# Seven-product up-projection: pads off POOL, sums a product ahead, another order of products, first weights loaded in the last output tile

## The chip, the cores and the metric

The kernel runs on one core of a Trainium2 chip. The metric is the device time of one execution in microseconds (us), the median of several runs. A core has TensorE (PE in the profile, with PEld for its weight loads), VectorE (DVE), ScalarE (ACT), GpSimd (POOL) and SyncE (SP, which here only issues DMAs). Each engine works through its own instructions in order and waits on semaphores for the others.

## The reference, cut to what matters

The kernel computes one layer of a hybrid decoder: a mixer (a state-space part and a convolution part side by side), then a gated MLP with a causal depthwise convolution of width 3. The change touches the last step of the mixer (its output projection) and the up-projection of the MLP.

```python
def rmsnorm(x, w):
    xf = x.astype(jnp.float32)
    r = lax.rsqrt(jnp.mean(xf * xf, axis=-1, keepdims=True) + EPS)
    return (xf * r).astype(x.dtype) * w
...
def conv_ffn(h, buf0, w_up, conv_w, conv_b, w_down):
    u = h @ w_up                                    # 2048 -> 2 x 5504
    u, buf = causal_dwconv(u, buf0, conv_w, conv_b) # width 3, along the tokens
    g, v = jnp.split(u, [FFN_DIM], axis=-1)
    return (jax.nn.silu(g) * v) @ w_down, buf
...
    out = jnp.concatenate([y.astype(h.dtype), u], axis=-1) @ w_out   # last step of mixer
...
        xp = xp + m
        f, p_ffc = conv_ffn(rmsnorm(xp, norm_ffn_w[i]), p_ffc0, *ffn_w)
        xp = xp + f
```

There are 544 tokens: 512 of one prompt and 8 x 4 of running samples. All is in float32.

## The kernel before

**Stages.** Input projection and mixer (to about 1015 us), the output projection of the first half (to 1217), of the second half, `ou`, in 16 tiles (to 1410.7), the up-projection (to 2425.6), and the down-projection. Every matmul stands for three: weights and activations are split into a high part (a cast, on ScalarE) and a low part (source minus high part, on VectorE), and TensorE runs high x high, high x low and low x high (L1246 to L1248 in the up-projection).

**Up-projection.** The hidden size has 43 groups (HID) of 128 columns of gate and 128 of value. A group is a 2 x 2 block problem (gate and value by the two halves of the input dimension, against the two halves of the tokens) worked with seven products in place of eight, each of 8 k-tiles x 3 passes = 24 matmuls with 272 columns. Product q = 7g+m wants a weight tile of 128x1024 and the operands T_t[m, k], which are sums of the normalised activations.

- *Weights.* `load_w(g, j)` loads five raw tiles a group, j = 0 to 4, each by one DMA of SP (L1198); j = 1 and 2 are sums of two blocks, so a second DMA, on POOL's queue, adds the other block once the first has landed (L1200). There are five buffers (`wr`). `prep_sum` makes the sixth tile, `ws` = raw 1 + raw 0 (L1211), and later adds raw 3 to it (L1213). `prep_h` casts a tile to its high part `sh` on ScalarE (L1221), `prep_l` makes the low part `sl` on VectorE (L1230); both have three buffers.
- *Operands.* `t_first` to `t_fourth` make T for one k: a split of the activations (`Ta`), of a difference (`tr`, L1130), of another (L1137), and of the second half (L1112, `Th` and `Tl`). For k = 0 to 4 (NPRE = 5) they run during the `ou` tiles, for k = 5, 6, 7 when the up-projection starts.
- *Behind a product.* `evac` adds its result from PSUM (four banks) into the group's tiles `c1`, `c2`, `pu`. `conv_task(g-1, m)` spreads the convolution of the group before over the seven iterations: at m = 0 and 2 `conv_in` for gate and value (two pads on POOL, L1279 and L1280; the normalisation factor `rr` or `nr` applied on VectorE, L1281 and L1282; the first tap on ScalarE, L1284), at 1 and 4 the other taps on VectorE, at 2 the silu on ScalarE, at 5 the product `ra` on VectorE and its store to DRAM (`ad`).

**What sets the order.** The order is written by hand: each engine's queue has the instructions in the order in which the loop over q emits them. An iteration before the change is

```python
            prep_sum(q + 2)
            prep_h(q + 2)
            if q:
                evac(q - 1)
            conv_task(q // 7 - 1, q % 7)
            prep_l(q + 2)
            ...
            product(q)
```

so the weights are prepared two products ahead. During the `ou` tiles, `delay(n, f)` and the steps that `ou_evac` returns place work between the weight blocks of the following tile; `swap` opens a pool of buffers in the place of one that is finished.

**The normalisation factor** of the MLP is not needed by the products. Its sum over the activations comes from a short TensorE step after the last `ou` tile; then `rv` (L243), a root, a reciprocal (L246) and three small steps follow on VectorE, before the first `conv_in` of the up-projection wants `rr`.

Of the kernel before, what the change touches and what calls it, by code (L numbers as in the profile page):

```python
# [9 lines left out]
F32R = mybir.dt.float32r  # L10
AF = mybir.ActivationFunctionType
ALU = mybir.AluOpType
# [4 lines left out]
KD = 16  # L17
HID = 43
KB = 4
NSLOT = 77  # L20
NSIDE = 10
CHUNKS = [14, 13, 12, 4]
U_SPILL = 8
# [6 lines left out]
def hymba_step_kernel(ctx: ExitStack, tc: tile.TileContext, a: dict):  # L30
# [236 lines left out]
    with tc.manual_schedule():  # L267
# [733 lines left out]
        def ln_gen():  # L1001
# [33 lines left out]
            def fin(t):  # L1035
                u = U_t.pop(t)

                def f1():
                    Uh[t] = slot("Uh", dt=F32R, side=t >= 12)
                    S.copy(Uh[t], u)  # L1040

                def f2():
                    Ul[t] = slot("Ul", dt=F32R, side=t >= 12)
# [83 lines left out]
        def t_second(k):  # L1127
            p, q = xs[k], xs[k + 8]
            r = tr[k] = slot("tr")
            V.tensor_tensor(r[:, 1, :], p[:, 0, :], p[:, 1, :], ALU.subtract)  # L1130
            V.scalar_tensor_tensor(r[:, 0, :], r[:, 1, :], -1.0, q[:, 1, :], ALU.mult, ALU.subtract)
            t_pair(k, r, (1, 2))

        def t_third(k):
            p, q = xs[k], xs[k + 8]
            r, s = tr.pop(k), slot("tr")
            V.tensor_tensor(s[:, 0, :], q[:, 1, :], p[:, 1, :], ALU.subtract)  # L1137
            V.scalar_tensor_tensor(s[:, 1, :], r[:, 0, :], -1.0, q[:, 0, :], ALU.mult, ALU.subtract)
            t_pair(k, s, (3, 6))

        def t_fourth(k):
            t_pair(k, xs.pop(k + 8), (4, 5))
            xs.pop(k)

        T_STEPS = [t_first, t_second, t_third, t_fourth]
        NPRE = 5

        def ou_evac(i):
            t = OT[i]

            def go(ps):
# [9 lines left out]
                def s1():  # L1161
# [7 lines left out]
                steps = [s0, s1]  # L1169
# [7 lines left out]
        run_jobs()  # L1177

        whl = swap("whl", "wp", bufs=1)
        wr = swap("wr", "side1", bufs=1, side="right")
        pst = swap("pst", "pmm", bufs=4, space=bass.MemoryType.PSUM)
        KW = 8 * 128
        fcw = cload("fcw", [128, 86, 4])
        fstate = []
        raw = {}

        def load_w(g, j):
            if g >= HID:
# [7 lines left out]
                G.dma_start(out=t, in_=more, accum_op=ALU.add)  # L1200
            raw[g, j] = t

        wq = {}

        def prep_sum(q):
            g, m = divmod(q, 7)
            if g >= HID:
                return
            if m == 1:
                raw[g, 5] = wr.tile([128, KW], F32, tag="s", bufs=1, name=nm("ws"))  # L1210
                V.tensor_tensor(raw[g, 5], raw[g, 1], raw[g, 0], ALU.add)  # L1211
            if m == 5:
                V.tensor_tensor(raw[g, 5], raw[g, 5], raw[g, 3], ALU.add)  # L1213

        def prep_h(q):
            g, m = divmod(q, 7)
            if g >= HID:
                return
            src = raw[g, (0, 5, 1, 2, 3, 5, 4)[m]]
            h = whl.tile([128, KW], F32R, tag="h", bufs=3, name=nm("sh"))  # L1220
            S.copy(h, src)  # L1221
            wq[q] = (src, h)

        def prep_l(q):
            g, m = divmod(q, 7)
            if g >= HID:
                return
            src, h = wq[q]
            l = whl.tile([128, KW], F32R, tag="l", bufs=3, name=nm("sl"))
            V.tensor_tensor(l, src, h.bitcast(F32), ALU.subtract)  # L1230
            wq[q] = (h, l)
            nxt = {1: (0,), 2: (1,), 3: (2,), 5: (3,), 6: (4,)}.get(m, ())
            for j in nxt:
                load_w(g + 1, j)

        bank = {}

# [14 lines left out]
        def evac(q):  # L1252
# [3 lines left out]
            c1, c2, pu = cg[g]  # L1256
            o = bank.pop(q)[:, 0:NH]
            if m == 0:
                S.copy(c1[:, 0, :], o)
            elif m == 1:  # L1260
                V.tensor_tensor(pu[:, 0, :], o, c1[:, 0, :], ALU.add)
            elif m == 2:
                V.tensor_tensor(pu[:, 1, :], o, pu[:, 0, :], ALU.add)
            elif m == 3:
                V.tensor_tensor(c2, o.unsqueeze(1).to_broadcast([128, 2, NH]), pu, ALU.add)
            elif m == 4:
                V.tensor_tensor(c1[:, 0, :], o, c1[:, 0, :], ALU.add)
# [24 lines left out]
        def conv_task(g, i):  # L1292
# [9 lines left out]
            elif i == 2:  # L1302
                o = cw[g][1]
                q = cw[g] = slot("gq", [128, 576])
                S.activation(q[:, 0:560], o[:, 0:560], AF.Silu)
                conv_in(HID + g, cg.pop(g)[1], R["nr2"])
            elif i == 4:
                conv_taps(HID + g)
# [7 lines left out]
                store(a_dram[g], flat(r))  # L1316

        NQ = 7 * HID
        for j in range(5):
            load_w(0, j)  # L1320
# [4 lines left out]
        rest = range(NPRE, 8)  # L1325
        for k in rest:
            if k == 7:
                prep_h(0)
                prep_l(0)
                drain_later()  # L1330
            t_first(k)
        prep_sum(1)
        for q in range(NQ):
            if q == 0:
                prep_h(1)
                prep_l(1)
                for k in rest:
                    t_second(k)
            tick()
            prep_sum(q + 2)  # L1340
            prep_h(q + 2)
            if q:
                evac(q - 1)
            conv_task(q // 7 - 1, q % 7)
            prep_l(q + 2)
            if q == 1:
                for k in rest:
                    t_third(k)
            if q == 2:
                for k in rest:  # L1350
                    t_fourth(k)
            product(q)
        evac(NQ - 1)
        T_t.clear()
# [273 lines left out]
```

## Time and profile before

| | before |
|---|---|
| median of 3 runs | 2981.86 us (2979.32 to 2982.01) |
| the profiled execution | 2978.53 us |
| its span | 2976.8 us |
| PE busy | 2875.1 us, 97% of the span |
| PEld busy | 2808.5 us, 94% |
| DVE busy | 1916.6 us, 64% |
| ACT busy | 1139.3 us, 38% |
| POOL busy | 902.3 us, 30% |
| weight loads of the up-projection, SP | 215 of 512 KB |
| accumulating weight loads, POOL | 86 of 512 KB |

A share of the span is a mean over stages: POOL's time lies for the most part ahead of the up-projection. Matmuls overlap in the array, so a matmul's own duration (about 0.29 us) is longer than its share of the time; how fast TensorE is going is read from how many start in a stretch. In rows of the trace the time in brackets is how long the engine stood idle ahead of the row, and what ended that.

### The profile page before, as it was taken

How to read it: one execution, taken by the hardware profiler on the slowest of the kernel's cores; microseconds unless marked ns; L12 is line 12 of the kernel's file. 1: busy time of each engine (PE TensorE's matmuls, PEld its weight loads, DVE VectorE, ACT ScalarE, POOL GpSimd, SP SyncE). 2: the span in 40 equal slices, each digit the busy share in tenths (PEclk: the TensorE clock that was granted, in tenths of full speed). 3: DMA queues.
4: the chain of work that ended last, by engine and by line, in shares of the span. 5: the costliest groups of instructions: out<-in, count | busy, mean ns of one | idle time of the engine just before them, and what ended most of it. 6: DMA issues, size and time to landing. Idle time of an engine off the chain costs nothing. (4 is left out here: it accounts for less than half of the span.)

```text
span 2976.8 us, 55786 instructions
## 1 busy us (share of the span) xinstructions
PE 2875.1 (97%) x22502; PEld 2808.5 (94%) x22502; DVE 1916.6 (64%) x2826; ACT 1139.3 (38%) x1682; POOL 902.3 (30%) x1068
## 2 busy tenths in 40 slices
PE   8999999999999999999899999999999989999997
PEld 8999999999999999999799999999999989999997
DVE  7576656777777874343777777777777774232334
ACT  5545434333333334233343434343434343232224
POOL 4567667666666655111001000010001000000003
PEclk9999999999999999999899999999999999999999
DMA  4243344333333344443566666676666655343421
GB/s 161 81 127 95 95 133 130 106 103 104 104 95 94 117 139 141 133 133 111 155 170 179 177 170 172 178 178 175 171 180 178 174 171 170 109 133 86 150 85 61
DMA packets 196677, 403.44 MB, mean 136 GB/s; under 512 B 38337, under 2 KB 47169, under 8 KB 196417
## 3 DMA queue, kind: packets, MB, share of 16 engines
q1 hardware_dynamic: 184032, 354.78, 38.7%
q0 software_dynamic: 12384, 45.09, 8.5%
q8 instruction: 176, 2.88, 0.4%
q14 instruction: 85, 0.69, 0.1%
HBM read 357.37 MB, written 42.41 MB: 134 GB/s over the span
## 5 line engine op out<-in xcount | busy, mean ns | idle before, releaser
L117 ACT CAST wh<-raw 128x512 fp32r<-128x512 f32 x592 | 355.6, 603 | 867.1 <-PE mm L228 735.0
L1248 PE MATMUL st<-Th,sl 128*128 128x272 f32 x2064 | 608.0, 295 | 32.6 <-DVE sl L1230 32.0
L1246 PE MATMUL st<-Th,sh 128*128 128x272 f32 x2064 | 604.1, 293 | 19.6 <-ACT sh L1221 17.6
L1247 PE MATMUL st<-Tl,sh 128*128 128x272 f32 x2064 | 599.6, 290 | 0.8 <-DVE Tl L1112 0.8
L118 POOL TENSOR_TENSOR wl<-raw,wh 128x512 fp32r<-128x512 f32 x336 | 449.4, 1340 | 416.9 <-ACT wh L117 356.5
L228 PE MATMUL mm<-xh,wh 128*128 128x272 f32 x2304 | 487.8, 293 | 7.3 <-ACT xh L312 7.3
L228 PE MATMUL mm<-xl,wh 128*128 128x272 f32 x2304 | 479.9, 289 | 3.2 <-DVE xl L314 3.2
L228 PE MATMUL mm<-xh,wl 128*128 128x272 f32 x2304 | 479.1, 289 | 0.0
L1248 PEld LDWEIGHTS st<-Th,sl 128*128 128x128 f32 x2064 | 391.8, 190 | 51.4 <-DVE sl L1230 51.2
L1246 PEld LDWEIGHTS st<-Th,sh 128*128 128x128 f32 x2064 | 391.9, 190 | 28.9 <-ACT sh L1221 27.2
L118 DVE TENSOR_TENSOR wl<-raw,wh 128x512 fp32r<-128x512 f32 (+2 forms) x256 | 181.2, 709 | 351.9 <-ACT wh L117 349.1
L1247 PEld LDWEIGHTS st<-Tl,sh 128*128 128x128 f32 x2064 | 392.2, 190 | 1.3 <-DVE Tl L1112 1.2
L228 PEld LDWEIGHTS mm<-xh,wh 128*128 128x128 f32 x2304 | 366.0, 189 | 20.0 <-issue 10.4
L228 PEld LDWEIGHTS mm<-xl,wh 128*128 128x128 f32 x2304 | 365.8, 189 | 4.1 <-DVE xl L314 4.0
L228 PEld LDWEIGHTS mm<-xh,wl 128*128 128x128 f32 x2304 | 366.1, 189 | 0.0
L1200 POOL DMA_DIRECT2D wr<-in_w_up x86 | 74.9, 871 | 899.7 <-DMA wr<-in_w_up 418.5
L937 DVE SCALAR_TENSOR_TENSOR ax<-w,cfw,ax 128x512 f32<-128x512 f32 x448 | 302.1, 746 | 5.8 <-ACT ax L913 5.8
L228 PE MATMUL mm<-Ah,wh 128*128 128x272 f32 x1248 | 260.0, 289 | 8.0 <-ACT Ah L1111 7.9
L1230 DVE TENSOR_TENSOR sl<-wr,sh 128x1024 fp32r<-128x1024 f32 x215 | 261.8, 1218 | 0.6 <-ACT sh L1221 0.6
L228 PE MATMUL mm<-Al,wh 128*128 128x272 f32 x1248 | 259.8, 289 | 0.0
L228 PE MATMUL mm<-Ah,wl 128*128 128x272 f32 x1248 | 259.7, 289 | 0.0
L1230 DVE TENSOR_TENSOR sl<-ws,sh 128x1024 fp32r<-128x1024 f32 x86 | 105.4, 1225 | 209.3 <-ACT sh L1221 209.3
(299 smaller groups left out, 5107.2 us busy)
## 6 DMA issues: line engine op xcount, KB each, us to landing
wr<-in_w_up SPq DMA_DIRECT2D x215, 512.0 KB, 3.9
raw<-in_w_in SPq DMA_DIRECT2D x292, 256.0 KB, 3.2
wr<-in_w_up POOLq DMA_DIRECT2D x86, 512.0 KB, 7.9
raw<-in_w_down SPq DMA_DIRECT2D x144, 256.0 KB, 2.7
raw<-in_w_out SPq DMA_DIRECT2D x128, 256.0 KB, 2.9
ad<-ra SPq DMA_DIRECT2D x43, 272.0 KB, 4.5
ar<-ad SPq DMA_DIRECT2D x43, 272.0 KB, 4.2
h<-in_h SPq DMA_DIRECT2D x32, 256.0 KB, 3.7
```

Source lines behind the costliest of these rows:

```text
L117: S.copy(h[:, :n], r[:, :n])
L118: (cur["wl"] or eng).tensor_tensor(l[:, :n], r[:, :n], h[:, :n].bitcast(F32), ALU.subtract)
L228: T.matmul(o, lhsT=w[:, c], rhs=x[:, hf, :], start=first, stop=last)
L937: V.scalar_tensor_tensor(p, w[:, i:i + 512], wt(i), p, ALU.mult, ALU.add)
L1200: G.dma_start(out=t, in_=more, accum_op=ALU.add)
L1230: V.tensor_tensor(l, src, h.bitcast(F32), ALU.subtract)
L1246: T.matmul(out, lhsT=h[:, c], rhs=xh_, start=k == 0, stop=False)
L1247: T.matmul(out, lhsT=h[:, c], rhs=xl_, start=False, stop=False)
L1248: T.matmul(out, lhsT=l[:, c], rhs=xh_, start=False, stop=k == 7)
```

## The change

Five things change. The pads of `conv_in` are a memset on VectorE and a copy on ScalarE, no longer on POOL. The two sums into `ws` are emitted behind `prep_l`, one iteration before the cast that reads them. The products of a group use the raw tiles in the order 0, 3, `ws`, 1, 2, `ws`, 4 (before: 0, `ws`, 1, 2, 3, `ws`, 4), with the operands and evictions renumbered, and the second `conv_in` goes from m = 2 to m = 3. The loads of the next group are issued at other places. In the last `ou` tile the weight buffers are opened on the place of another pool (`side0`, for which the layer norm's tiles are finished in another order), the five first loads are issued there, and the operands for k = 5 and 6 are made there.

```diff
-            for t in range(16):
+            for t in list(range(U_SPILL, 16)) + list(range(2, U_SPILL)) + [0, 1]:
+                if t == 0:
+                    Cur.side = swap("side0", "side1", bufs=4, side="right")
                 fin(t)
...
                 if i + 1 < 16:
                     load_xr(i + 1)
+                else:
+                    delay(0, up_open)
+                    delay(0, lambda: (t_first(5), t_fourth(5)))
+                    delay(1, lambda: (t_second(5), t_third(5)))
+                    delay(1, lambda: (t_first(6), t_fourth(6)))
+                    delay(2, lambda: (t_second(6), t_third(6)))
...
-            t_pair(k, r, (1, 2))
+            t_pair(k, r, (2, 3))
...
+        def up_open():
+            nonlocal wr
+            wr = swap("wr", "side0", bufs=1, side="right")
+            for j in (0, 1, 3, 2, 4):
+                load_w(0, j)
...
-            if m == 1:
+        def sum_a(g):
+            if g < HID:
                 raw[g, 5] = wr.tile([128, KW], F32, tag="s", bufs=1, name=nm("ws"))
                 V.tensor_tensor(raw[g, 5], raw[g, 1], raw[g, 0], ALU.add)
-            if m == 5:
-                V.tensor_tensor(raw[g, 5], raw[g, 5], raw[g, 3], ALU.add)
+                load_w(g + 1, 0)
+
+        def sum_b(g):
+            V.tensor_tensor(raw[g, 5], raw[g, 5], raw[g, 3], ALU.add)
+            load_w(g + 1, 3)
...
-            src = raw[g, (0, 5, 1, 2, 3, 5, 4)[m]]
+            src = raw[g, (0, 3, 5, 1, 2, 5, 4)[m]]
...
-            nxt = {1: (0,), 2: (1,), 3: (2,), 5: (3,), 6: (4,)}.get(m, ())
-            for j in nxt:
-                load_w(g + 1, j)
+            if m in (3, 4, 6):
+                load_w(g + 1, {3: 1, 4: 2, 6: 4}[m])
...
-            G.memset(w[:, 0:2], 0.0)
-            G.tensor_copy(ws[:, :, 0:2], fstate[t // 29][:, t % 29, :].rearrange("p (b x) -> p b x", x=2))
+            V.memset(w[:, 0:2], 0.0)
+            S.copy(ws[:, :, 0:2], fstate[t // 29][:, t % 29, :].rearrange("p (b x) -> p b x", x=2))
...
+            elif i == 3:
                 conv_in(HID + g, cg.pop(g)[1], R["nr2"])
...
         for q in range(NQ):
+            g, m = divmod(q, 7)
+            tick()
             if q == 0:
-                prep_h(1)
+                t_fourth(7)
                 prep_l(1)
-                for k in rest:
-                    t_second(k)
-            tick()
-            prep_sum(q + 2)
+                t_second(7)
+                sum_a(0)
             prep_h(q + 2)
             if q:
                 evac(q - 1)
-            conv_task(q // 7 - 1, q % 7)
+            conv_task(g - 1, m)
             prep_l(q + 2)
             if q == 1:
-                for k in rest:
-                    t_third(k)
-            if q == 2:
-                for k in rest:
-                    t_fourth(k)
+                t_third(7)
+                xs.clear()
+            if m == 2:
+                sum_b(g)
+            if m == 6:
+                sum_a(g + 1)
             product(q)
```

How the instructions stand on three engines, before and after. On ScalarE, in a steady group, from the eviction of a product to the casts behind the second convolution's first tap (`gq` is the silu, `o` the convolution, `w` its padded input), before:

```order
L1259 COPY c_18711<-st_18684 128x272
L1221 CAST sh_18747<-wr_18539 128x1024
L1305 ACTIVATE gq_18750<-o_18673 128x560
L1284 ACTIVATE o_18753<-w_18752,fcw_16760 128x560
L1221 CAST sh_18788<-ws_18634 128x1024
L1221 CAST sh_18820<-wr_18573 128x1024
```

and with the change:

```order
L1263 COPY pu_18460<-st_18430 128x272
L1226 CAST sh_18494<-wr_18247 128x1024
L1309 ACTIVATE gq_18497<-o_18422 128x560
L1226 CAST sh_18533<-ws_18389 128x1024
L1284 COPY w_18536<-fs_16875 128x8x2
L1288 ACTIVATE o_18537<-w_18536,fcw_16871 128x560
L1226 CAST sh_18570<-wr_18323 128x1024
```

The cast of the second `ws` now stands ahead of the first tap `o`, where it stood behind it, and the pad's copy stands in ScalarE's own queue.

On VectorE, in a steady group, around the first sum, from the product `ra` of the group before on, before:

```order
L1314 TENSOR_TENSOR ra_18858<-gq_18750,o_18753 128x2x256
L1315 TENSOR_TENSOR ra_18858<-gq_18750,o_18753 128x2x16
L1230 TENSOR_TENSOR sl_18861<-wr_18641,sh_18855 128x1024
L1211 TENSOR_TENSOR ws_18888<-wr_18681,wr_18641 128x1024
L1269 TENSOR_TENSOR c_18711<-st_18863,pu_18713 128x272
L1230 TENSOR_TENSOR sl_18893<-ws_18888,sh_18890 128x1024
L1271 TENSOR_TENSOR c_18712<-st_18897,c_18712 128x272
L1281 TENSOR_TENSOR w_18926<-c_18711,rr_17005 128x512
L1282 TENSOR_TENSOR w_18926<-c_18711,rr_17005 128x8x4
```

and with the change:

```order
L1319 TENSOR_TENSOR ra_18608<-gq_18497,o_18537 128x2x256
L1320 TENSOR_TENSOR ra_18608<-gq_18497,o_18537 128x2x16
L1235 TENSOR_TENSOR sl_18611<-wr_18391,sh_18605 128x1024
L1273 TENSOR_TENSOR c_18458<-st_18613,pu_18460 128x272
L1235 TENSOR_TENSOR sl_18641<-wr_18505,sh_18638 128x1024
L1213 TENSOR_TENSOR ws_18643<-wr_18466,wr_18391 128x1024
L1275 TENSOR_TENSOR c_18459<-st_18647,c_18459 128x272
L1283 MEMSET w_18675 128x2
L1285 TENSOR_TENSOR w_18675<-c_18458,rr_17011 128x512
L1286 TENSOR_TENSOR w_18675<-c_18458,rr_17011 128x8x4
L1235 TENSOR_TENSOR sl_18682<-ws_18643,sh_18672 128x1024
L1294 SCALAR_TENSOR_TENSOR o_18676<-w_18675,fcw_16871,o_18676 128x560 x2
```

The sum was followed at once by the split `sl<-ws` that needs it by way of ScalarE; now an eviction and a convolution's first steps stand between, and the split of raw 0 precedes the sum.

On SP, at the end of the `ou` tiles (`xs` are stores of the residual, `fcw` and `fs` the convolution's weights and states), before:

```order
L179 DMA xs_179<-xres_16250 128x544
L179 DMA xs_172<-xres_16380 128x544
L89 DMA fcw_16760<-in_fcw 128x344
L1198 DMA wr_16805<-in_w_up 128x1024
L1198 DMA wr_16807<-in_w_up 128x1024
L1198 DMA wr_16810<-in_w_up 128x1024
L1198 DMA wr_16813<-in_w_up 128x1024
L1198 DMA wr_16815<-in_w_up 128x1024
L1324 DMA fs_16817<-in_ffn_state 128x464
```

and with the change:

```order
L179 DMA xs_179<-xres_16297 128x544
L1205 DMA wr_16722<-in_w_up 128x1024
L1205 DMA wr_16724<-in_w_up 128x1024
L1205 DMA wr_16727<-in_w_up 128x1024
L1205 DMA wr_16729<-in_w_up 128x1024
L1205 DMA wr_16732<-in_w_up 128x1024
L179 DMA xs_172<-xres_16427 128x544
L89 DMA fcw_16871<-in_fcw 128x344
L1337 DMA fs_16873<-in_ffn_state 128x464
```

The five weight loads moved ahead of one store and of the convolution weights.

## Rows read from the trace of the kernel before

**Rows 1.** Busy times by stretch: length, each engine (instructions), clock, DMA share, GB/s.

```profile
1410.75:1461.30 50.55, 34.36 (x178) 31.30 (x178) 33.17 (x47) 17.65 (x25) 4.68 (x6) 0.76 0.57 155
1461.30:2425.60 964.30, 923.88 (x7057) 897.57 (x7055) 751.61 (x1051) 394.59 (x462) 90.20 (x252) 1.00 0.66 171
2402.70:2425.60 22.90, 22.90 (x182) 22.69 (x181) 18.06 (x26) 8.65 (x10) 2.14 (x4) 1.00 0.13 38
```

**Rows 2.** TensorE's waits from 1461.3 to 2425.6: total us, times, longest.

```profile
PE st L1248 <- DVE sl L1230: 28.9, 39, 0.7
PE st L1246 <- ACT sh L1221: 10.2, 27, 0.8
```

**Rows 3.** Timeline around the wait at 1824: start, us, engine, line [idle before].

```profile
1820.89 0.51 POOL L1280 COPY w<-fs 128x16 f32<-128x16 f32 x1
...
1821.28 0.85 ACT L1284 ACTIVATE o<-w,fcw 128x560 f32<-128x560 f32 x1 [6.15 <-POOL w L1280]
...
1822.04 1.03 ACT L1221 CAST sh<-ws 128x1024 fp32r<-128x1024 f32 x1
...
1824.38 0.40 PE L1248 MATMUL st<-Th,sl 128*128 128x272 f32 x1 [0.74 <-DVE sl L1230]
```

**Rows 4.** Timeline of the last group, 2412 to 2421.

```profile
2413.09 0.86 ACT L1284 ACTIVATE o<-w,fcw 128x560 f32<-128x560 f32 x1 [1.04 <-issue]
...
2418.25 1.63 DVE L1290 SCALAR_TENSOR_TENSOR o<-w,fcw,o 128x560 f32<-128x560 f32 x2
...
2419.80 1.22 DVE L1230 TENSOR_TENSOR sl<-wr,sh 128x1024 fp32r<-128x1024 f32 x1
```

**Rows 5.** Timeline of TensorE at the start of the up-projection.

```profile
1413.92 0.59 PE L1246 MATMUL st<-Ta,sh 128*128 128x272 f32 x1 [3.17 <-ACT sh L1221]
...
1426.25 0.59 PE L1246 MATMUL st<-Th,sh 128*128 128x272 f32 x1 [5.86 <-ACT sh L1221]
...
1456.80 0.40 PE L1248 MATMUL st<-Th,sl 128*128 128x272 f32 x1 [1.87 <-DVE sl L1230]
...
1461.06 0.30 PE L1248 MATMUL st<-Th,sl 128*128 128x272 f32 x1
```

**Rows 6.** Timeline of VectorE at the start of the up-projection.

```profile
1400.80 0.69 DVE L118 TENSOR_TENSOR wl<-raw,wh 128x512 fp32r<-128x512 f32 x1 [1.33 <-ACT wh L117]
...
1410.79 0.72 DVE L1156 TENSOR_TENSOR xres<-mm,xres 128x544 f32<-128x544 f32 x1 [9.30 <-PE mm L228]
...
1413.90 1.23 DVE L1230 TENSOR_TENSOR sl<-wr,sh 128x1024 fp32r<-128x1024 f32 x1 [0.47 <-ACT sh L1221]
...
1423.84 1.22 DVE L1211 TENSOR_TENSOR ws<-wr,wr 128x1024 f32<-128x1024 f32 x1 [8.36 <-DMA wr<-in_w_up]
...
1427.37 0.44 DVE L1130 TENSOR_TENSOR tr<-xs 128x272 f32<-128x272 f32 x1
...
1429.64 0.43 DVE L1130 TENSOR_TENSOR tr<-xs 128x272 f32<-128x272 f32 x1
...
1444.66 1.99 DVE L1112 TENSOR_TENSOR Tl<-xs,Th 128x544 fp32r<-128x544 f32 x3
...
1446.57 0.78 DVE L243 TENSOR_SCALAR rv<-ax 128x272 f32<-128x272 f32 x2
```

**Rows 7.** VectorE's one memset: us in total, mean ns, idle before.

```profile
L304 DVE MEMSET ones<- 128x128 f32 x1 | 0.2, 165 | 0.8 <-PEq L1617 0.8
```

**Rows 8.** L1198 and then L1200, 1500 to 2400: landing times and issue ns.

```profile
DMA to landing us min/median/max: 3.5/3.9/9.7
...
L1200 POOL DMA_DIRECT2D wr<-in_w_up x78: 862/865/888, 1517.4 to 2393.8; - x78
...
DMA to landing us min/median/max: 6.6/8.0/9.5
```

**Rows 9.** Timeline of SP's queue at the end of the last output tile.

```profile
1400.40 12.16 SPq L1198 DMA_DIRECT2D wr<-in_w_up  x5
```

**Rows 10.** The layer norm's step on `U`: ns min/median/max, first and last start.

```profile
L1045 DVE TENSOR_TENSOR U<-U,rr x16: 708/1261/1889, 1108.2 to 1153.7; 128x544 f32<-128x544 f32 x16
```

More of the change, by code (lines that the diff above doesn't have):

```diff
@@ L19 @@
 KB = 4
-NSLOT = 77
+NSLOT = 76
 NSIDE = 10
@@ L1038, in f1 @@
                 def f1():
-                    Uh[t] = slot("Uh", dt=F32R, side=t >= 12)
+                    Uh[t] = slot("Uh", dt=F32R, side=t < 2)
                     S.copy(Uh[t], u)
                 def f2():
-                    Ul[t] = slot("Ul", dt=F32R, side=t >= 12)
+                    Ul[t] = slot("Ul", dt=F32R, side=t < 2)
                     V.tensor_tensor(Ul[t], u, Uh[t].bitcast(F32), ALU.subtract)
@@ L1138, in t_third @@
             V.scalar_tensor_tensor(s[:, 1, :], r[:, 0, :], -1.0, q[:, 0, :], ALU.mult, ALU.subtract)
-            t_pair(k, s, (3, 6))
+            t_pair(k, s, (4, 6))
         def t_fourth(k):
-            t_pair(k, xs.pop(k + 8), (4, 5))
-            xs.pop(k)
-        T_STEPS = [t_first, t_second, t_third, t_fourth]
+            t_pair(k, xs[k + 8], (1, 5))
+        T_STEPS = [t_first, t_fourth, t_second, t_third]
         NPRE = 5
@@ L1168, in s1 @@
                         spawn(rsqrt_gen([fst["acc"], sq], setr("r2")), 3)
-                steps = [s0, s1]
+                steps = [s0, s1] if i < 15 else [lambda: None, s0, s1]
                 if i % 2 and i // 2 < NPRE:
@@ L1176, in hymba_step_kernel @@
             job("ou", out_srcs(OT[i], 1), lambda k: (Uh[k], Ul[k]), ou_evac(i), V, ou_pre(i))
[L1177 to L1185, printed above, removed]
         KW = 8 * 128
-        fcw = cload("fcw", [128, 86, 4])
-        fstate = []
-        raw = {}
+        raw, wq, wr = {}, {}, None
+        def up_open():
[3 more added lines that the diff above has]
+                load_w(0, j)
         def load_w(g, j):
@@ L1201, in load_w @@
             raw[g, j] = t
[L1203 to L1208, printed above, removed]
-            if m == 1:
+        def sum_a(g):
+            if g < HID:
                 raw[g, 5] = wr.tile([128, KW], F32, tag="s", bufs=1, name=nm("ws"))
                 V.tensor_tensor(raw[g, 5], raw[g, 1], raw[g, 0], ALU.add)
-            if m == 5:
-                V.tensor_tensor(raw[g, 5], raw[g, 5], raw[g, 3], ALU.add)
+                load_w(g + 1, 0)
+        def sum_b(g):
+            V.tensor_tensor(raw[g, 5], raw[g, 5], raw[g, 3], ALU.add)
+            load_w(g + 1, 3)
         def prep_h(q):
@@ L1258, in evac @@
             if m == 0:
-                S.copy(c1[:, 0, :], o)
+                S.copy(pu[:, 0, :], o)
             elif m == 1:
-                V.tensor_tensor(pu[:, 0, :], o, c1[:, 0, :], ALU.add)
+                V.tensor_tensor(c1[:, 0, :], o, pu[:, 0, :], ALU.add)
             elif m == 2:
+                V.tensor_tensor(pu[:, 0, :], o, pu[:, 0, :], ALU.add)
+            elif m == 3:
                 V.tensor_tensor(pu[:, 1, :], o, pu[:, 0, :], ALU.add)
-            elif m == 3:
+            elif m == 4:
                 V.tensor_tensor(c2, o.unsqueeze(1).to_broadcast([128, 2, NH]), pu, ALU.add)
-            elif m == 4:
-                V.tensor_tensor(c1[:, 0, :], o, c1[:, 0, :], ALU.add)
             elif m == 5:
@@ L1318, in hymba_step_kernel @@
         NQ = 7 * HID
-        for j in range(5):
-            load_w(0, j)
+        run_jobs()
+        whl = swap("whl", "wp", bufs=1)
+        pst = swap("pst", "pmm", bufs=4, space=bass.MemoryType.PSUM)
+        prep_h(0)
+        prep_l(0)
+        drain_later()
+        t_first(7)
+        prep_h(1)
+        fcw = cload("fcw", [128, 86, 4])
+        fstate = []
         for i in range(3):
@@ L1324, in hymba_step_kernel @@
             Y.dma_start(out=fstate[i][:, 0:n, :], in_=a["ffn_state"][:, 29 * i:29 * i + n, :])
-        rest = range(NPRE, 8)
-        for k in rest:
[L1327 to L1332, printed above, removed]
         for q in range(NQ):
+            g, m = divmod(q, 7)
+            tick()
             if q == 0:
-                prep_h(1)
+                t_fourth(7)
                 prep_l(1)
-                for k in rest:
-                    t_second(k)
-            tick()
-            prep_sum(q + 2)
+                t_second(7)
+                sum_a(0)
             prep_h(q + 2)
@@ L1343, in hymba_step_kernel @@
                 evac(q - 1)
-            conv_task(q // 7 - 1, q % 7)
+            conv_task(g - 1, m)
             prep_l(q + 2)
             if q == 1:
-                for k in rest:
-                    t_third(k)
-            if q == 2:
-                for k in rest:
-                    t_fourth(k)
+                t_third(7)
[4 more added lines that the diff above has]
+                sum_a(g + 1)
             product(q)
```

## The prediction

> **What bounds the kernel now.** I read first the busy times of stretches, because TensorE is the bound nearly everywhere and a mean over the span hides where it is not. Product 6 of group 0 issues its last matmul at 1461.06 [rows 5]; from there to 2425.6, in 42 groups, TensorE issues 42 x 168 = 7056 matmuls in 964.3 us, 22.96 us a group [rows 1]. In the last group, which has no further weights to load, 182 matmuls fill 22.90 us without a gap, 0.1258 us each [rows 1]. At that rate a group needs 21.14 us and the 7056 need 887.8. So the stretch **loses 76.5 us**, 1.82 a group. The chip grants the full clock there (1.00, its 2.4 GHz level) [rows 1].
>
> The waits of TensorE say for what: 28.9 us (39 times) for the low part of a weight tile from VectorE, 10.2 us (27 times) for the high part from ScalarE [rows 2]. They sum to 39.1, about half of the count's loss; the other half has no row of its own, and I take it to be the restart behind each stop and the clock that follows it. The count is what I use, and the other reading is a rival below.
>
> Next, one stop along the chain. At 1824.38 TensorE waits 0.74 for `sl` of the low pass [rows 3]. ScalarE cast the high part `sh<-ws` at 1822.04 only, because it had stood 6.15 us in front of the first step of the second convolution, which waits for POOL [rows 3]. POOL ran that pad copy at 1820.89 [rows 3]: its queue is in order, and an accumulating weight DMA ahead of it had first to see the plain load land. ScalarE's cast is late, VectorE's subtraction is late, TensorE stops. The cross-check is the last group, where POOL has no DMA left: the same step of ScalarE waited 1.04, and for nothing that the profile shows [rows 4].
>
> **The transition.** Group 0 costs 50.55 us for the first window, of which TensorE is busy 34.36 at a clock of 0.76 between the two levels [rows 1]. Its stops are 3.17 at the start, 5.86 before product 1 and 1.87 at the end, among smaller ones [rows 5]. VectorE's rows tell why: it sits 8.36 us until the accumulated weight tile lands at 1423.84, then makes the operands for k=5, 6, 7 one after another (second steps 2.27 us apart, 1427.37 to 1429.64), and reaches `rv` only at 1446.57 [rows 6]; the `sl` of product 6, behind the reciprocal that follows `rv`, lets TensorE go on at 1456.80 [rows 5].
>
> **The change, part by part, steady groups.** (1) Pads: POOL loses a memset and a copy per convolution and keeps only DMA issues. VectorE gets two memsets a group, at most 0.165 us each by the larger 128x128 one [rows 7]; ScalarE two copies, each below the 0.85 us of the much larger 128x560 activation [rows 3]. ScalarE is busy 394.59 / 42 = 9.4 us a group and VectorE 751.61 / 42 = 17.9 [rows 1]; they become at most 11.1 and 18.2 of 21.14. Both stay under TensorE, which hides them. Without that cover the two memsets would cost 0.33 us a group, 14 us in all. What stood behind POOL's DMA wait is now behind nothing: the cast `sh<-ws` follows in ScalarE's order only an activation whose operands VectorE has made. (2) Sums one product ahead: in one iteration ScalarE no longer waits for the sum it is to cast; same instructions, another place, so no price. (3) The second convolution's start moves from iteration 2 to 3, to even VectorE out. The longest iteration becomes the one with two taps: taps to the end of the next split take 2.77 us from 2418.25 [rows 4], with an eviction of 0.35 to 0.43 ahead (an estimate from the spacing of 128x272 steps [rows 6]) 3.1, against 3.02 a product. VectorE leads by two products, so the others (about 2.3 to 2.7) make it up: I find no split that is ready less than about 2.9 us before its product. The 76.5 should go wholly; I keep 15 us of it back for the range.
>
> (4) Later loads. The load of the second block comes after its split in iteration 1, one product later than before, and the first sum is wanted earlier. Counting from the end of product 0: load issued at 2.5 (two taps and a split, some 2.7, begun a little earlier), landing 3.9 (3.5 to 9.7), POOL's issue 0.87, accumulation landing 8.0 (6.6 to 9.5) [rows 8]: there at 15.2. The sum is wanted at 17.4 (five products, 15.1, and an eviction and a split behind them); TensorE suffers only if it begins after 21.8 (product 2 of the next group starts at 8 x 3.02 = 24.2, and sum and cast take 2.3). That leaves 6.6 us at the medians; if all worst cases met, 2.5 + 9.7 + 0.9 + 9.5 = 22.6, late by 0.8. VectorE is busy 78% of the stretch now [rows 1], and the landing times were measured beside that; it will be 86%. A rule speaks against the change here: the Trainium skill, "SBUF — State Buffer", section "SBUF: two separate sides", warns that descriptors which POOL writes can starve while VectorE holds the port they share. By that rule the accumulation would land later the busier VectorE is, and the last rival would be the likelier case, with its time. No row shows a starved issue (862 to 888 ns [rows 8]), and by the rows the cost is nothing.
>
> **The transition after.** The first weights are issued after one store in the last output tile, not over 12.16 us from 1400.40 on, where SP waited for buffers [rows 9]; the order shows five loads ahead of the store, the convolution weights and the states. Operands for k=5 and 6 are made in the last output tile, where VectorE has run its last weight step at 1400.80 and idles until 1410.79 [rows 6]. Four second and third steps at 2.27 and two short ones, some 11.4 us from 1401.5, end about 1413, so this does not quite fit: product 0 starts near 1413.0 (now 1413.92 [rows 5]), its low part near 1414.3. From the first split (1413.90) to `rv` (1446.57) VectorE now takes 32.7 us [rows 6]. Off come the wait of 8.36, four steps of 2.27 = 9.1, and two of the three last splits, 2 x 0.66 = 1.3 (1.99 for three [rows 6]); on come what is now behind the first split, the tile's eviction and the split of k=7, 3.1 to 3.6 (1410.79 to 1413.90 [rows 6]). That gives 17.0 to 17.5, with late ends up to 19: the first split starts near 1413.2, so `rv` near 1430.5 to 1432.5. From `rv`'s start to TensorE's release it is 10.2 now [rows 5, 6], and then 4.5 to the end of product 6: about 1446, against 1461.3. **Gain 15 us** (11 to 17; at the very most 50.55 - 21.14 = 29, were group 0 gapless). The layer norm's tiles are finished in another order, for the buffers: the same sixteen steps, over at 1153.7 [rows 10], tens of us before that tile order is read. POOL's queue gets the accumulation of the first blocks about 10 us earlier; behind it there stands only a square sum. The store and the constants now behind the weight loads on SP have some 40 us until their first use.
>
> **The sum.** The profiled run's span is 2976.8 and 1.7 lie around it (2978.5). 2976.8 - 76.5 - 15 + 1.7 = 2887. This run was 3.3 below the median of those shown (2981.86), so 2890.
>
> **The rivals.** (a) *Only the waits go.* If the half of the loss without a row is not restarts but, say, transfers that slow matmuls in all groups with loads, 39.1 + 15 go: 2928. A sum that is late by 0.3 to 1.2 us a group ends in the same place (2905 to 2940). For it: the gapless rate comes from one group without loads. Against it: the loss sits in groups that have waits, and short stops with slow first matmuls are seen in the transition [rows 5]. 0.10. (b) *The change does not do what it says*: VectorE, at 86%, takes the place of POOL and the splits remain as late; only the transition gains: 2967. Against it, the last group runs gapless with 18.06 of 22.90 us on VectorE [rows 1]. 0.05. (c) *Neither*: the splits stay late, and the operand steps ahead of product 0 also eat the transition's gain: within 6 us of 2982. 0.02. (d) *Slower: the accumulation lands too late.* The first sum waits at the head of VectorE's queue, with evictions and splits behind it. From the load's issue to the landing 19.3 us are free; to be slower than before each group must lose over 91.5 / 42 = 2.2 us, a route of over 21.5 us against 12.8 at the medians and 20.1 with all maxima [rows 8]. At 23 us in every group it would be about 3.7 a group, 3045. 0.03.
>
> **How the numbers follow.** My forecast, gapless steady groups and a shorter transition, has 0.80 and its own range, 2876 (group 0 gapless too) to 2906 (15 us of stops stay). The range of 8 in 10 takes in the nearer half of (a) and a run's spread: 2874 to 2918. A measurement of this kernel can tell about 0.2%, 6 us, from no change. Faster: 0.80 + 0.10 + 0.05 = 0.95; same 0.02; slower 0.03.
>
> **What would show it.** Right: in the steady stretch, TensorE's waits for `sl` and `sh` are near nothing and 7056 matmuls take about 888 us; ScalarE has no POOL wait at the convolution's first step; VectorE's first sum does not wait for a DMA; product 6 of group 0 ends near 1446. (a) shows as waits gone and matmuls above 0.13 us in groups with loads; (b) as waits for `sl` with VectorE busy all through; (d) as VectorE idle before the first sum, released by a DMA. What would make me wrong is the operand chain in the last output tile, whose place beside that tile's own steps I only estimate.

## The result and the profile after

The changed kernel takes **2892.36 us** (median of 4, 2890.37 to 2895.56) against 2981.94 (2979.32 to 2982.75): the ratio is 0.9702, with a 95% interval of 0.9685 to 0.9719. The forecast was 2890 in a range of 2874 to 2918. The profiled run took 2892.68 with a span of 2890.9, so the two profiled spans differ by 85.9 us.

First the busy times by stretch in the trace of the changed kernel (length, then each engine with its instructions, granted clock, DMA share, GB/s): group 0, then the 42 steady groups, then the last of them.

```profile
1415.90:1450.20 34.30, 28.01 (x177) 26.72 (x177) 26.14 (x34) 15.38 (x20) 1.74 (x2) 0.85 0.60 159
1450.20:2339.60 889.40, 889.10 (x7059) 888.82 (x7057) 772.70 (x1136) 424.21 (x545) 71.28 (x82) 1.00 0.70 186
2316.00:2338.90 22.90, 22.90 (x184) 22.90 (x183) 17.32 (x27) 8.56 (x12) 0.00 (x0) 1.00 0.18 54
```

These compare with [rows 1]. Group 0 has become 34.3 us from 50.55, and the steady groups 889.4 from 964.3. The count of matmuls in the steady groups is the same 7056 plus a few at the edges, and at 0.12582 us each they need 887.8: of the 76.5 us lost before, 1.6 are left. TensorE's waits in that stretch are down to one row, where [rows 2] had 66 waits:

```profile
PE st L1252 <- DVE sl L1235: 0.3, 1, 0.3
```

POOL's part in the kernel before shows in two rows that were not given so far. The first is POOL's second accumulating DMA, just ahead of the pad of [rows 3]: it stood 2.38 us, and what came last was by the trace the store of `ra`, 0.7 us after the plain load. The second sums the waits of ScalarE's first tap for POOL over the steady groups (us in total, times, longest); the changed kernel has no such row.

```profile
1820.14 0.86 POOL L1200 DMA_DIRECT2D wr<-in_w_up  x1 [2.38 <-DMA ad<-ra]
...
ACT o L1284 <- POOL w L1280: 238.5, 41, 6.5
```

The groups of instructions that took the place of POOL's pads (us in total, mean ns of one, idle time ahead): ScalarE's copy and the convolution's first tap, and VectorE's memset.

```profile
L1288 ACT ACTIVATE o<-w,fcw 128x560 f32<-128x560 f32 x86 | 73.7, 857 | 6.6 <-DVE w L1286 3.5 <-ACT w L1284 0.2
...
L1284 ACT COPY w<-fs 128x16 f32<-128x16 f32 x86 | 17.2, 200 | 0.0
...
L1283 DVE MEMSET w<- 128x2 f32 x86 | 5.2, 60 | 0.0
```

The copy is 200 ns, the memset 60. The first tap, which had stood 6.15 us in front of POOL in [rows 3], waits 6.6 us in all 86 instances together, and for nothing on POOL.

At the start of the up-projection the timelines answer to [rows 5, 6, 9]. TensorE:

```profile
1419.25 0.59 PE L1250 MATMUL st<-Ta,sh 128*128 128x272 f32 x1 [3.33 <-ACT sh L1226]
...
1430.69 0.39 PE L1250 MATMUL st<-Th,sh 128*128 128x272 f32 x1 [1.45 <-ACT sh L1226]
...
1450.32 0.29 PE L1250 MATMUL st<-Ta,sh 128*128 128x272 f32 x1
```

VectorE, from the first operand step of k=5 in the last output tile to `rv`, and SP's weight loads:

```profile
1406.82 1.46 DVE L1120 TENSOR_TENSOR Ta<-xs,Ta 128x272 fp32r<-128x272 f32 x1 [0.18 <-ACT Ta L1119]
...
1418.28 0.73 DVE L1120 TENSOR_TENSOR Tl<-tr,Th 128x544 fp32r<-128x544 f32 x1 [0.77 <-ACT Th L1119]
1419.23 1.23 DVE L1235 TENSOR_TENSOR sl<-wr,sh 128x1024 fp32r<-128x1024 f32 x1 [0.22 <-ACT sh L1226]
...
1428.34 1.22 DVE L1213 TENSOR_TENSOR ws<-wr,wr 128x1024 f32<-128x1024 f32 x1
...
1437.71 0.43 DVE L243 TENSOR_SCALAR rv<-ax 128x272 f32<-128x272 f32 x1
```

```profile
1392.92 14.16 SPq L1205 DMA_DIRECT2D wr<-in_w_up  x5
```

Operand steps run from 1406.82 to 1419.0, then the first split; SP's five loads go out from 1392.92 on, spread over 14.16 us, so that they too waited on the way; the sum at 1428.34 has no wait for a DMA in front of it, where 8.36 us stood [rows 6]; `rv` comes at 1437.71. But the whole timeline is late: the `ou` tiles end at 1415.9 here, 5.1 us later than before. The same shift is there already where TensorE waits for the layer norm's sum (L1031), ahead of which no instruction changed; the kernel before, then the changed one:

```profile
1095.39 2.18 PE L238 MATMUL ax<-va,ones 128*128 128x272 f32 x4 [6.31 <-DVE va L1031]
```

```profile
1100.44 2.18 PE L238 MATMUL ax<-va,ones 128*128 128x272 f32 x4 [6.32 <-DVE va L1031]
```

So the two spans should differ by 74.9 (steady groups) + 16.3 (group 0) - 5.1 (something ahead of 1100 us), 86.1 in all, and 85.9 were measured. The 5.1 were in no part of the prediction.

### The profile page after: what moved, and what is told of

It is laid out like the page before. It is cut to its first block, busy times and chain, and to the rows that moved or that the text cites. A ratio compares the mean times of both kernels' runs of the same rounds, so it can differ in the third digit from the quotient of the medians.

```text
span 2890.9 us, 55668 instructions
## 1 busy us (share of the span) xinstructions
PE 2837.0 (98%) x22502; PEld 2796.8 (97%) x22502; DVE 1933.7 (67%) x2912; ACT 1170.8 (40%) x1768; POOL 882.5 (31%) x896
## 5 line engine op out<-in xcount | busy, mean ns | idle before, releaser
L1250 PE MATMUL st<-Th,sh 128*128 128x272 f32 x2064 | 596.1, 289 | 1.5 <-ACT sh L1226 1.5
L1252 PE MATMUL st<-Th,sl 128*128 128x272 f32 x2064 | 595.8, 289 | 1.1 <-DVE sl L1235 1.1
L228 PEld LDWEIGHTS mm<-xh,wh 128*128 128x128 f32 x2304 | 365.6, 189 | 20.5 <-issue 10.4
L1226 ACT CAST sh<-wr 128x1024 fp32r<-128x1024 f32 x215 | 225.4, 1049 | 272.6 <-PE st L1251 262.2
L1207 POOL DMA_DIRECT2D wr<-in_w_up x86 | 74.9, 871 | 828.9 <-DVE pu L1267 534.3
```

Of the source, the lines that this page charges most:

```text
L228: T.matmul(o, lhsT=w[:, c], rhs=x[:, hf, :], start=first, stop=last)
L1250: T.matmul(out, lhsT=h[:, c], rhs=xh_, start=k == 0, stop=False)
L1252: T.matmul(out, lhsT=l[:, c], rhs=xh_, start=False, stop=k == 7)
```

## The experiments

Each kernel ran with the kernel before on the same chip, whose medians in the three sets were 2983.18, 2983.75 and 2982.06. The first question was which part of the change the steady groups' 75 us hang on.

**Pads alone.** In the kernel before:

```diff
-            G.memset(w[:, 0:2], 0.0)
-            G.tensor_copy(ws[:, :, 0:2], fstate[t // 29][:, t % 29, :].rearrange("p (b x) -> p b x", x=2))
+            V.memset(w[:, 0:2], 0.0)
+            S.copy(ws[:, :, 0:2], fstate[t // 29][:, t % 29, :].rearrange("p (b x) -> p b x", x=2))
```

> The kernel before with one edit: the two pads of the convolution go to VectorE and ScalarE. Theory A (the stall of a group needs two things at once, the pad behind a DMA wait in POOL's queue and the cast of the weight sum behind that pad's reader in ScalarE's): taking away the first is enough, 7056 matmuls take about 890 us, the start stays as it was, so 2982 - 75 = 2907 (2902 to 2914). Rival B (the pads alone matter): the same 2907. Rival C (the sums matter, a sum in the iteration of its own cast makes the split late): only part goes, 2940 to 2960, with waits for the split of the sum left.

Measured: 2905.32 us (2904.8 to 2905.97), ratio 0.974 (0.9726 to 0.9755). The steady groups run without a stop, as this stretch of its trace shows, with the sums still in the iteration of their casts; the changed kernel's same stretch follows, with 18 matmuls more:

```profile
1500.00:2300.00 800.00, 800.00 (x6336) 800.00 (x6336) 688.00 (x1018) 382.24 (x492) 66.11 (x76) 1.00 0.72 190
```

```profile
1500.00:2300.00 800.00, 800.00 (x6354) 800.00 (x6353) 696.02 (x1022) 382.74 (x492) 66.11 (x76) 1.00 0.72 191
```

All 42 steady groups take 892.8 us here, against 964.3 before and 889.4 in the changed kernel.

**Pads back on POOL.** In the changed kernel:

```diff
-            V.memset(w[:, 0:2], 0.0)
-            S.copy(ws[:, :, 0:2], ...)
+            G.memset(w[:, 0:2], 0.0)
+            G.tensor_copy(ws[:, :, 0:2], ...)
```

> The changed kernel with the pads put back on POOL, all else as changed. Theory A: the reordering alone is enough or nearly so. Counted from the end of product 0, POOL's pad of the second convolution is done at about 11.5, behind two accumulating DMAs; the first tap at 12.4, the next cast 13.4, two taps 13.9, the split 15.1, wanted at 15.1: 0 to 0.3 us a group lost, 2892 to 2905. Rival B (pads alone matter): the stall of the kernel before comes back at another product, 1.2 to 1.8 us a group, 2942 to 2968. Rival C: 2892 to 2900.

Measured: 2975.92 (2974.57 to 2978.29), ratio 0.9977 (0.9968 to 0.9987). Theory A, and C with it, fell: with the sums ahead and the other order of products nearly all is lost again, 2.0 us a group more than the changed kernel. Rival B named the kind of stop, but the loss is above its range too (1.2 to 1.8 a group, at most 2968). The timelines of POOL, ScalarE, VectorE and TensorE in this run show where:

```profile
1816.74 0.86 POOL L1207 DMA_DIRECT2D wr<-in_w_up  x1 [3.17 <-DMA wr<-in_w_up]
...
1817.49 0.51 POOL L1284 COPY w<-fs 128x16 f32<-128x16 f32 x1
```

```profile
1811.28 1.05 ACT L1226 CAST sh<-ws 128x1024 fp32r<-128x1024 f32 x1 [2.21 <-DVE ws L1217]
1817.88 0.85 ACT L1288 ACTIVATE o<-w,fcw 128x560 f32<-128x560 f32 x1 [5.55 <-POOL w L1284]
```

```profile
1818.77 1.64 DVE L1294 SCALAR_TENSOR_TENSOR o<-w,fcw,o 128x560 f32<-128x560 f32 x2 [4.76 <-ACT o L1288]
1820.32 1.22 DVE L1235 TENSOR_TENSOR sl<-wr,sh 128x1024 fp32r<-128x1024 f32 x1
```

```profile
1821.60 0.39 PE L1252 MATMUL st<-Th,sl 128*128 128x272 f32 x1 [1.35 <-DVE sl L1235]
```

POOL's second accumulating DMA waits 3.17 us for its load; the pad behind it lets the first tap go at 1817.88, 5.55 late. The cast of the sum is ahead of that now, as intended. But the two taps stand ahead of the next split in VectorE's queue and wait 4.76, and TensorE stops 1.35 us for that split. The expectation's estimate failed at the pad's time: it is done at 1818.0, 13.7 us after the end of product 0 and not 11.5, because POOL's second accumulating DMA waits for a load that landed later than counted.

**Pads on POOL, but early.** In the kernel before, both pairs of pads of a group go to m = 0, ahead of the group's accumulating DMAs (`conv_pad` holds the two POOL instructions):

```diff
+                conv_pad(g)
+                conv_pad(HID + g)
                 conv_in(g, cg[g][0], R["r2"])
```

> The kernel before with the pads still on POOL, but both pairs of a group issued together at m = 0, ahead of the accumulating DMAs of that group. If only the place in POOL's queue behind a DMA wait is at fault: the steady groups run gapless as with the pads off POOL, 2905 (2902 to 2909). Rival (POOL itself is slow or is slowed by VectorE's use of memory, 0.43 and 0.52 us a pad): half of the loss stays, 2935 to 2960.

Measured: 2905.74 (2905.29 to 2907.85), ratio 0.974 (0.9727 to 0.9753), the same as with the pads off POOL. Its stretch of the trace has POOL busier than in the run above and TensorE as full:

```profile
1500.00:2300.00 800.00, 800.00 (x6336) 800.00 (x6335) 687.02 (x943) 370.49 (x416) 94.59 (x226) 1.00 0.73 190
```

So it was not POOL's work that cost, but its place behind a DMA's wait.

**The start.** The changed kernel with its start undone: weights, operands of k=5, 6, 7, layer norm and 77 slots as before, in the new order of products:

```diff
-                    delay(0, up_open)
-                    delay(0, lambda: (t_first(5), t_fourth(5)))
...
-                t_fourth(7)
+                for k in rest:
+                    t_fourth(k)
                 prep_l(1)
-                t_second(7)
+                for k in rest:
+                    t_second(k)
                 sum_a(0)
```

> The changed kernel with the start of the up-projection as before: weights loaded and the operands of k=5, 6, 7 made after the last output tile, in the new order of products. Theory T (VectorE's operand steps count in full): group 0 ends 16 us later, 2908 (2905 to 2911). Theory W (half of the gain came from the wait for the accumulated tile, which the new order of products hides behind operand steps anyway): about 8 us later, 2900 (2897 to 2904).

Measured: 2899.65 (2898.7 to 2901.16), ratio 0.9721 (0.9705 to 0.9737), where theory W was. But the comparison was not clean, because of the slots (below): against a kernel with 77 slots too, the start is worth 11.8 us, between the two theories; 10.4 of them lie between the layer norm's sum and the end of group 0. In the trace of this run the longest stop left is one behind operand steps, where a DMA's landing had been:

```profile
1432.80 0.59 PE L1242 MATMUL st<-Th,sh 128*128 128x272 f32 x1 [6.06 <-ACT sh L1218]
```

**A shorter chain.** The changed kernel with second and third steps of k=6 behind the first split, and `sum_a(0)` ahead of `t_first(7)`:

```diff
-                    delay(2, lambda: (t_second(6), t_third(6)))
...
         drain_later()
+        sum_a(0)
         t_first(7)
...
-                t_second(7)
-                sum_a(0)
+                t_second(6)
+                t_second(7)
...
+                t_third(6)
                 t_third(7)
```

> The changed kernel with a shorter chain ahead of product 0: second and third operand steps of k=6 go behind the first split, and the first sum ahead of the operands of k=7, where VectorE waits for ScalarE. If the chain of VectorE sets the start: product 0 begins about 3 us earlier and product 2 about 2.5, 2889.5 (2888 to 2891.5). Rival: the later products are held by the low clock after the stop or the sum waits for its accumulated tile, and what is won is given back: 2892 to 2895.

Measured: 2892.24 (2889.83 to 2893.6), ratio 0.9696 (0.9681 to 0.971); against the changed kernel it can't be told apart. Its first product waits 0.93 instead of 3.33, but the split of product 6, behind the reciprocal, now comes late:

```profile
1415.16 0.39 PE L1249 MATMUL st<-Ta,sh 128*128 128x272 f32 x1 [0.93 <-ACT sh L1225]
...
1444.57 0.40 PE L1251 MATMUL st<-Th,sl 128*128 128x272 f32 x1 [1.03 <-DVE sl L1234]
```

Counted from TensorE's wait for the layer norm's sum, group 0 ends 0.7 us earlier. The rival held in part: what was won at the start was given back, though to a stop and not to a DMA.

**The accumulated tile's lead.** The load of raw tile 1 placed one iteration later in the loop, and three later:

```diff
-            if m in (3, 4, 6):
-                load_w(g + 1, {3: 1, 4: 2, 6: 4}[m])
+            for j in {4: (1, 2), 6: (4,)}.get(m, ()):       # one late
+            for j in {4: (2,), 6: (1, 4)}.get(m, ()):       # three late
+                load_w(g + 1, j)
```

> The changed kernel with the load of raw tile 1 one iteration later, 3.0 us. In its trace the accumulated tile lands about 1.5 us before the sum and the sum could wait some 4.5 more before TensorE runs dry, 6.0 in all: VectorE waits a little for the DMA, TensorE not, 2892 (2889 to 2897). Rival (a wait at the head of VectorE's queue costs at once, because evictions and splits stand behind it): 0.3 to 1 us a group, 2905 to 2935.

> The changed kernel with the load of raw tile 1 three iterations later, about 9 us, 3 more than the 6.0 that are free: 2 to 3.5 us a group lost, 42 groups, 2976 to 3040, and VectorE's first sum waits for the DMA in every group. Rival (the DMA lands sooner when it does not share its time with two other loads, and VectorE's lead takes up the rest): under 1 us a group, 2895 to 2930.

Measured: one late 2892.07 (2890.0 to 2892.78), ratio 0.9692 (0.9679 to 0.9705); three late 2994.14 (2988.08 to 3001.45), ratio 1.0036 (1.0026 to 1.0046), slower than the kernel before by 0.4%.

The first of the two did not do what its expectation says. SP takes its own instructions in order, and nothing stands in its queue between the two places of that load; by the traces each of the five engines runs the same operations on the same tiles in the same order as in the changed kernel. Three loads of the group leave together, in the changed kernel and then with "one late":

```profile
1816.22 4.50 SPq L1205 DMA_DIRECT2D wr<-in_w_up  x3
```

```profile
1816.26 3.86 SPq L1205 DMA_DIRECT2D wr<-in_w_up  x3
```

At the median the first of them leaves 2.59 us after the end of product 0 in both. So this run repeats the changed kernel, and a delay of 3 us stays untried. With three late the load does move: it goes out behind two other loads and a store, 8.0 us later, and POOL's accumulation of raw 2 now stands ahead of that of raw 1.

The waits of VectorE with one late, then of VectorE and TensorE with three late (us in total, times, longest):

```profile
DVE ws L1213 <- DMA wr<-in_w_up: 1.1, 3, 0.5
```

```profile
DVE ws L1213 <- DMA wr<-in_w_up: 200.8, 41, 6.5
...
PE st L1250 <- ACT sh L1226: 35.4, 33, 2.7
PE st L1252 <- DVE sl L1235: 26.1, 37, 0.7
```

Three iterations cost 101.8 us, 2.4 a group: VectorE waits 4.9 at a time in 41 groups, and the stop reaches TensorE by way of the cast and the split.

**The slot.** The full diff of the change begins with a line that the section on the change leaves out: it takes a buffer away from the pool of general tiles (NSLOT 77 to 76). The changed kernel with 77; for room `ws` lies in the pool of the split weights, and two pools of the down-projection open in the other order:

```diff
-NSLOT = 76
+NSLOT = 77
-                raw[g, 5] = wr.tile([128, KW], F32, tag="s", bufs=1, name=nm("ws"))
+                raw[g, 5] = whl.tile([128, KW], F32, tag="s", bufs=1, name=nm("ws"))
```

> The changed kernel with 77 slots instead of 76; for room the weight sum's buffer lies in the pool of the split weights. The runs with 76 slots reach the layer norm's sum 3.5 to 8 us later, counted from the mixer's start, than those with 77. If the slot is the cause: 2887.5 (2885 to 2890). Rival (spread between runs): 2892 (2890 to 2895).

Measured: **2887.81** (2886.77 to 2888.66), ratio 0.9679 (0.9665 to 0.9692), the fastest of all. And the pads-only kernel with 76 slots:

```diff
-NSLOT = 77
+NSLOT = 76
```

> The kernel of e1 (only the pads off POOL) with 76 slots instead of 77. If one slot less costs 4.5 us ahead of the up-projection, whatever the rest of the kernel: 2909.8 (2907.5 to 2912). Rival (the slot's price in the changed kernel came from the other pool of the weight sum): 2905 (2904 to 2907).

Measured: 2909.84 (2908.63 to 2912.02), ratio 0.976 (0.9747 to 0.9774), 4.5 above the same kernel with 77. The timelines of TensorE in the mixer, with 77 slots in the changed kernel and with 76 in the pads-only one:

```profile
473.14 0.66 PE L655 MATMUL ax<-MT,xdt 128*64 128x128 f32 x8 [0.58 <-DVE seg L633]
...
1095.72 2.18 PE L238 MATMUL ax<-va,ones 128*128 128x272 f32 x4 [6.27 <-DVE va L1031]
```

```profile
474.80 1.11 PE L655 MATMUL ax<-MT,xdt 128*64 128x128 f32 x8 [1.94 <-DVE seg L633]
...
1098.36 2.18 PE L238 MATMUL ax<-va,ones 128*128 128x272 f32 x4 [6.29 <-DVE va L1031]
```

A step of the state-space part waits 1.94 for VectorE with 76 slots and 0.58 with 77. The twelve traces divide by the slot alone: with 76 this wait is 1.81 to 1.95 and the layer norm's sum on TensorE starts at 1098.3 to 1103.0; with 77 the wait is 0.59 at most, and the sum starts at 1094.5 to 1097.0. Part of the rest is TensorE's clock. In five of the six traces with 76 slots the granted clock is at its 1.2 GHz level for 3.4 or 6.8 us in the mixer, as here in the pads-only kernel right behind that stop; with 77 it never is.

```profile
474.90:478.30 3.40, 3.40 (x29) 3.07 (x30) 2.84 (x5) 1.14 (x3) 3.40 (x4) 0.50 0.10 16
```

**All together.** The kernel of the slot experiment with the shorter chain, and the normalisation factor's chain two iterations later:

```diff
-                        spawn(rsqrt_gen([fst["acc"], sq], setr("r2")), 3)
+                        spawn(rsqrt_gen([fst["acc"], sq], setr("r2")), 5)
```

> The kernel of e8 with the order of e4 at the start (second and third operand steps of k=6 behind the first split, first sum earlier) and with the normalisation factor's chain two iterations later, so that the reciprocal no longer stands ahead of the split of product 6. In e4 the start was 4 us earlier and the end of group 0 only 1, with a stop of 1.03 before product 6. If the reciprocal took the rest: 2887.8 - 2.5 = 2885.3 (2883.5 to 2887). Rival (the low clock behind the start's stops, or the same chain a group later, takes it): 2887 to 2889.

Measured: 2888.85 (2888.05 to 2891.48), ratio 0.9689 (0.9676 to 0.9702): the rival's range, and no gain over the slot alone (2887.81). Counted from the layer norm's sum, group 0 ends 1.7 us earlier than with the slot alone, and in group 1, where the reciprocal now stands, TensorE waits for a split:

```profile
PE st L1251 <- DVE sl L1234: 2.3, 1, 2.3
```

## Why the prediction was right

**The sum.** The forecast span was 2976.8 - 76.5 - 15 = 2885.3, the measured one 2890.9. The 5.6 between them are 1.6 (steady groups) - 1.3 (transition) + 5.1 (a term that was not there), and 0.2 elsewhere. That the medians are only 2.4 apart is luck in part: the forecast had 3.3 added because the profiled run before lay that much below its median, while the profiled run after lay 0.3 above its own.

- *The count, not the waits* (76.5): 74.9 came. The half of the loss that had no row of its own went with the waits, so rival (a) is out, and reading matmuls against the gapless rate sized the stage better than adding up the waits (39.1). Where that half sat can be read from the starts of the matmuls around the stop of [rows 3], at 1824.38, in the kernel before, and from the waits of the weight loads in its steady groups:

```profile
1823.35 0.29 PE L1247 MATMUL st<-Tl,sh 128*128 128x272 f32 x1
1824.38 0.40 PE L1248 MATMUL st<-Th,sl 128*128 128x272 f32 x1 [0.74 <-DVE sl L1230]
1824.62 0.29 PE L1246 MATMUL st<-Th,sh 128*128 128x272 f32 x1
```

```profile
PEld st L1248 <- DVE sl L1230: 47.0, 79, 1.0
PEld st L1246 <- ACT sh L1221: 19.4, 39, 1.1
```

  From the first of these starts to the last, 0.25 us would have been the gapless rate, and it took 1.27: 1.02 are lost where the row says 0.74, because the row counts only from the shown end of the matmul ahead, which lasts 0.29, and because the next start comes 0.24 after the first one. Added up so over the steady groups, the 66 stops with a row lost 49.7 us, 52 short ones that only the weight loads show 9.6, and the starts right behind the 118 stops 12.5. The clock, which the prediction named beside the restart, accounts for 2.9: the 1.00 of [rows 1] is rounded, and behind stops at 1500.53 and 1707.86 the granted clock stood at the 1.2 GHz level for 3.4 us each time. All other starts are at the gapless rate but for 1.7 us in all.
- *The chain behind it* (pad behind a DMA wait, tap, cast, split): right for the cause. Pads alone give 77.9 us in the medians, early pads on POOL 78.0. Of the 74.9 in the two traces, pads alone give 71.5 (964.3 to 892.8). The sums ahead and the new order add about 3 once the pads are free: 890.1 with the start undone, 889.4 in the changed kernel, and a group without a stop takes 21.16 us in place of 21.22. Why, no run here shows. The prediction gave the sums no price and no gain of their own, which holds but for these 3; my theory in the experiments, that they alone would do, did not.
- *Rival (b), VectorE as the new bound*: it is busy 772.70 / 42 = 18.4 us a group, 0.2 above the bound given, 87% of the stretch, and TensorE does not wait for it. The lead of two products is enough.
- *The later load*: counted from the end of product 0, at the median, the load left at 2.6, the tile landed at 16.1 and the sum began at 17.4 (2.5, 15.2 and 17.4 forecast). The lead is 1.3 us at the median and 0.02 at the least, and VectorE never waits for that landing. With three iterations more the tile landed at 24.8, 3.0 beyond the 21.8 that the prediction named as the limit; it cost 2.4 us a group, a little over the 2.2 at which rival (d) turns the sign. So (d) is a real mechanism and its price about right, and the change stays clear of it. Landing took 9.2 us at the median, not 8.0; the rows are of the changed kernel, then of the pads alone:

```profile
L1207 POOL DMA_DIRECT2D wr<-in_w_up x76: 862/865/888, 1503.5 to 2289.5; - x76
...
DMA to landing us min/median/max: 7.9/9.2/10.7
```

```profile
L1200 POOL DMA_DIRECT2D wr<-in_w_up x76: 862/865/891, 1509.7 to 2298.6; - x76
...
DMA to landing us min/median/max: 5.8/7.5/8.8
```

  The rule weighed in the prediction (the Trainium skill, "SBUF — State Buffer", section "SBUF: two separate sides") is about operations that VectorE runs in a mode with two ports; the prediction stretched it to all of VectorE's load. The runs don't bear that out: the issue stays at 862 to 891 ns, and with the pads alone, VectorE at 86%, the landing is 7.5. The order of loads alone does not explain it either: with the pads back on POOL three loads leave together just the same, and the median is 7.8. What goes with the landing in all twelve traces is how many other DMAs of SP and POOL are in flight beside it, 1.8 to 2.1 on average where it takes 7.3 to 7.9 us and 3.1 to 3.4 where it takes 9.1 to 9.3. No run changed that number by itself, so the cause stays argued.
- *The transition* (15): 16.3. Less the 5.1 of shift, the operand chain ran from 1401.7 to 1413.9 (1401.5 to 1413 forecast), `rv` came at 1432.6 (1430.5 to 1432.5) and group 0 ended at 1445.1 (1446). The parts are told apart by the traces with 77 slots, from the layer norm's sum to the last matmul of group 0: 365.7 us before, 364.4 with pads alone, 359.8 with the new order as well, 349.4 with first weights and operands in the last tile. So the new order gives 4.5 (the accumulated tile's wait hidden) and the last tile's work 10.4.
- *The missing term*: NSLOT. The line stands in the full diff, and the prediction priced only the layer norm's order beside it. One slot less costs 4.5 us in two kernels (2892.36 against 2887.81, 2909.84 against 2905.32). It is small beside the range, but the prediction's account of the layer norm ("the same sixteen steps") left it out.

## What to carry to other kernels

Look at what stands behind a waiting instruction on each in-order queue: pads of half a microsecond behind a DMA's wait cost some 77 us, and it was as good to move them ahead of the DMA on the same engine as to give them to others. Size a stage by its work at the gapless rate, taken from a stretch without stops, since the waits of the matmul rows showed only 39.1 of the 76.5 us that the stops cost here. After an edit that moves an issue, look whether the queue really changed: a load placed later in the program left at the same time. A buffer count in a diff is an edit like any other: it acts wherever that pool is tight, here several hundred microseconds ahead of the code that wanted the room.

## What the runs showed of the hardware that was not expected

A stop of TensorE costs more than its matmul row shows: 39.1 us of waits before the change stood for 76.5 us. The rows of the weight loads came closer (66.4 us, 118 stops), and the start right behind a stop came about 0.23 us after the one before it, not 0.126. An accumulating DMA that POOL issues takes 862 to 891 ns of POOL in every run, with VectorE busy 77% to 87% of the stretch. It lands in 7.3 to 7.9 us at the median with 1.8 to 2.1 other DMAs of SP and POOL in flight beside it, and in 9.1 to 9.3 with 3.1 to 3.4; that is seen over twelve traces and was not tested by itself.
